# A recurrent mixer moved into a build-time plan, its conditioning sums moved from TensorE to VectorE

## The chip, the cores and the metric

One NeuronCore of a Trainium2 chip runs the whole program. The metric is the time of one execution in device microseconds; several executions give a median. The engines are named as in the profile: PE is TensorE's matmuls, PEld its weight loads, DVE is VectorE, ACT is ScalarE, POOL is GpSimd, SP is SyncE, which issues most of the transfers (DMAs) in one queue.

## The reference

Two transformer layers over 512 tokens of width 1024, in fp32. Layer 0 has a gated linear recurrence (HGRN2) as its mixer, layer 1 dilated attention; each layer then has a SwiGLU feed-forward. Six vectors per layer, computed from a conditioning vector, shift, scale and gate the normalised inputs and the outputs. Cut to what the change touches:

```python
cond = silu(c)                                             # [1, 1024]
for layer in range(2):
    mod = cond @ ada_w[layer] + ada_b[layer]               # [1, 6 * 1024]
    sh1, sc1, g1, sh2, sc2, g2 = split(mod, 6)             # vectors 0 to 5
    u = rms_norm(h, norm_g[layer, 0]) * (1 + sc1) + sh1
    y = hgrn2_mixer(u, ...) if layer == 0 else dilated_attention_mixer(u, ...)
    h = h + (1 + g1) * rms_norm(y, norm_g[layer, 1])
    u = rms_norm(h, norm_g[layer, 2]) * (1 + sc2) + sh2
    h = h + (1 + g2) * rms_norm(swiglu_ffn(u, ...), norm_g[layer, 3])

def hgrn2_mixer(u, w_in, lb, norm_g, w_out):               # 8 heads of 128, chunks of 32 tokens
    q_raw, f_raw, v, g = (u @ w_in) in four parts
    log_f = log(lb + (1 - lb) * sigmoid(f_raw)); k = (1 - lb) * sigmoid(-f_raw); q = silu(q_raw)
    b = cumsum(log_f within a chunk)
    o = tril((q * exp(b)) @ (k * exp(-b)).T) @ v + (q * exp(b)) @ state    # state decays from chunk to chunk
    return (rms_norm(o) * norm_g * silu(g)) @ w_out
```

## The kernel before

Weights come from HBM as a list of items (`items`), each about 1 MB, into "raw" tiles of 128 x 2048 fp32. The `Stream` class loads them in the list's order on SP's queue; two raw tiles take turns, so a load waits until the work on the item two places ahead is done. A weight item ("w") is split into a high part (a cast on ACT, L113) and a low part (a subtraction on DVE, L114), and every product is three matmuls (high x high, low x high, high x low; L599 to L601). Three pairs of such parts ("hi", "lo") are kept.

Between the weights the list has conditioning items ("ada"): half of the rows (`kq`) of a 512-column half (`hf`) of one vector `v` of layer `l`. During the recurrent mixer the list has 18 of them, for vectors (0, 2), (0, 4), (0, 3), (1, 4) and half of (1, 1). They are worked off in one of two ways:

- on TensorE, `ada_groups` (L386), for layer 0's vectors 2, 3 and 4: four matmuls of a 128 x 32 block of the conditioning vector, one for each quarter of the array's columns (L395), into a PSUM bank, which ACT copies to SBUF at the end (L399);
- on DVE, `ada_chunk` (L402), for the others: four instructions per item, each a chunk of 128 x 512 times a column of the conditioning vector, added to a sum in SBUF (L415 for the first, L417 for the rest).

The sum over the partitions is then taken by a matmul with ones (`sum_by_pe`: L444, L462) or by a GpSimd reduction, and "do" and "rows" items finish the vector.

The recurrent mixer starts once the values of all tokens are projected. For each of four pairs of heads it runs blocks of 128 output columns: two for the forget gate (sigmoids, L1631 and L1633), two for the query (L1641, L1642), and, for the pair before, two for the output gate (`gate_pair`, L1615 to L1618). Between the blocks come the steps of the recurrence, put off by a count of blocks (`Fillers`, `LAG`):

- `decays`: two scans on DVE (L1519, L1520) and products with them (L1523, L1524);
- `between` and `widened`: small products of decays, `ki` and `m64` on DVE (L1543, L1548, L1549), `k128` and `q128` on GpSimd (L1547, L1550);
- `core_a` to `core_d`: scores and mask, states of the chunks, outputs and their norm, and a transpose into `oT`.

Here the order on each engine is left to the framework's scheduler, which works from the program's order. Then `mixer_out` (L721) projects `oT` with the output weights: with `made=None` it opens the tiles for the high parts, cuts each head of `oT` in two (L594, L595) and runs the products of the first 512 columns for all tokens. From there on the order is written out by hand (`manual_schedule`).

The attention mixer of layer 1 is built in another way: its work is a list of tasks with an engine, a cost in us, and the names that they read and write (`Plan`, L164). `Plan.run` (L260) works out when each task is due, plays through 72 rules of choice, takes the one in which TensorE ends first, and emits the instructions in that order, which the engines then keep. There all conditioning is on DVE, the raw tiles are a place with two buffers, and the first products of the output projection are part of the plan.

Of the kernel before, what the change touches and what calls it, by code (L numbers as in the profile page):

```python
# [11 lines left out]
F32 = mybir.dt.float32  # L12
# [33 lines left out]
class Stream:  # L46
# [17 lines left out]
    def _load(self, i):  # L64
# [251 lines left out]
def block_kernel(tc, x, c, positions, ada_w, ada_b, norm_g, hgrn_w_in, lower, hgrn_norm_g, hgrn_w_out,  # L316
# [8 lines left out]
    with ExitStack() as ctx:  # L325
# [57 lines left out]
        by_pe = lambda l, v, hf: l == 0 and v in (2, 3, 4)  # L383
        sum_by_pe = lambda l, v, hf: by_pe(l, v, hf) or (l, v) == (1, 4) or (l, v, hf) == (1, 1, 0)

        def ada_groups(l, v, hf, kq):  # L386


            def run(raw):
                if kq == 0:  # L390
                    accs[l, v, hf] = bank("mm")
                ps, r = accs[l, v, hf], V4(raw)
                for k in range(4):
                    j = slice(32 * k, 32 * k + 32)
                    pe.matmul(ps[j], cond_tiles[:, kq * 4 + k], r[:, k], start=kq == 0, stop=kq == 1,  # L395
                              tile_position=(0, 32 * k))
                if kq == 1:
                    accs[l, v, hf] = acc_place()
                    act.copy(accs[l, v, hf], ps)  # L399
            return run  # L400

        def ada_chunk(l, v, hf, kq):  # L402
            if by_pe(l, v, hf):
                return ada_groups(l, v, hf, kq)

# [126 lines left out]
        items += weave(hg, own[:16] + [one[0], own[17] + one[1]], 1, 0.6) + hg_o[:1] + one[3][:1] + hg_o[1:]  # L532
        f0a, f0b = ffn_ws(0)
# [953 lines left out]

        otp = hx.enter_context(tc.tile_pool(name="h_ot", bufs=1))
# [5 lines left out]
        sc = cx.enter_context(tc.tile_pool(name="h_briefest", bufs=1))  # L1494
# [16 lines left out]
        bc = lambda a: a.unsqueeze(3).broadcast_to((P, 4, a.shape[2], 32))  # L1511

        def decays(hd, k, K, Q, dec):

            T = factors[k]
            act.activation(C33(T)[:, :, 1:33], C33(T)[:, :, 1:33], AF.Identity, scale=omlb[:, hd:hd + 1], bias=lb[:, hd:hd + 1])
            act.activation(K, K, AF.Copy, scale=omlb[:, hd:hd + 1])
            bb, suf = fresh(sc, [P, 528], "bb", 1), fresh(sc, [P, 528], "suf", 1)
            dve.tensor_tensor_scan(bb, T[:, 0:528], starts[:, 0:528], 0.0, op0=OP.mult, op1=OP.add)  # L1519
            dve.tensor_tensor_scan(suf[:, ::-1], T[:, 1:529][:, ::-1], starts[:, 1:529][:, ::-1], 0.0, op0=OP.mult, op1=OP.add)  # L1520
            dve.tensor_copy(dec[:, k], C33(bb)[:, :, 32])
            qd = fresh(sb, [P, S], "qd", 2)
            dve.tensor_mul(C16(qd), C33(bb)[:, :, 1:33], C16(Q))  # L1523
            dve.tensor_mul(C16(K), C33(suf)[:, :, 1:33], C16(K))  # L1524
            return qd, K

        def between(dec):

            d = dec.rearrange("p k (b c) -> p (k b) c", c=4)
            rdec = fresh(cp, [P, 2, 16], "rdec", 2)  # L1530
            dve.reciprocal(rdec, dec)
            dve.tensor_copy(reach[:, :, 1:7:5], d[:, :, 0:4:3])
            dve.tensor_mul(reach[:, :, 2:6:3], d[:, :, 0:3:2], d[:, :, 1:4:2])
            dve.tensor_mul(reach[:, :, 3:5], reach[:, :, 2:6:3], d[:, :, 2:0:-1])
            tot = fresh(cp, [P, 8, 1], "ftot", 2)
            dve.tensor_mul(tot, reach[:, :, 4:5], d[:, :, 0:1])
            dve.tensor_copy(f64[:, :, 0:4:3], d[:, :, 1:3])
            return rdec, tot

        def widened(hd, k, qd, ke, rdec, tot):  # L1540
            own = slice(4 * k, 4 * k + 4)
            ki = fresh(sc, [P, S], "ki", 2)
            dve.tensor_tensor(C16(ki), C16(ke), rdec[:, k].unsqueeze(2).broadcast_to((P, 16, 32)), op=OP.mult)  # L1543
            q128 = fresh(cp, [P, S], "q128", 2)
            k128 = fresh(sb, [P, S], "k128", 2)
            m64 = fresh(sc, [P, S], "m64", 2)
            pool.tensor_tensor(B44(k128), B44(ke), bc(reach[:, own, 4:8]), op=OP.mult)  # L1547
            dve.tensor_tensor(B44(m64)[:, :, 0:2], B44(ke)[:, :, 0:2], bc(f64[:, own, 0:2]), op=OP.mult)  # L1548
            dve.tensor_tensor(B44(m64)[:, :, 2:4], B44(qd)[:, :, 2:4], bc(f64[:, own, 2:4]), op=OP.mult)  # L1549
            pool.tensor_tensor(B44(q128), B44(qd), bc(reach[:, own, 0:4]), op=OP.mult)  # L1550
            return dict(qd=qd, ki=ki, ke=ke, q128=q128, k128=k128, m64=m64, tot=tot[:, own], hd=hd)

        def core_a(g):
            a = bank("a")
            qd, ki, ke, m64 = g["qd"], g["ki"], g["ke"], g["m64"]
            for o in range(0, S, P):
                pe.matmul(a[:, o:o + P], ki[:, o:o + P], qd[:, o:o + P], start=True, stop=True)
            for o in range(0, S, P):
                for s in (0, 64):
                    pe.matmul(a[s:s + 32, o + s + 32:o + s + 64], ke[:, o + s:o + s + 32],  # L1560
                              qd[:, o + s + 32:o + s + 64], start=True, stop=True, tile_position=(0, s))
            for o in range(0, S, P):
                pe.matmul(a[0:64, o + 64:o + P], m64[:, o:o + 64], m64[:, o + 64:o + P], start=True, stop=True,
                          tile_position=(0, 0))
            aT = fresh(cp, [P, NT, P], "aT", 2)
            dve.tensor_tensor(aT, V4(a), causal.unsqueeze(1).broadcast_to((P, NT, P)), op=OP.mult)
            g["aT"] = aT
            kb = bank("a")
            for b in range(NT - 1):
                pe.transpose(kb[:, b * P:(b + 1) * P], g["k128"][:, b * P:(b + 1) * P], ident)  # L1570
            act.copy(g["k128"][:, 0:384], kb[:, 0:384])

        def core_b(g):
            hs = slice(g["hd"] * P, (g["hd"] + 1) * P)
            kv = bank("b")
            for b in range(NT - 1):
                pe.matmul(kv[:, b * P:(b + 1) * P], g["k128"][:, b * P:(b + 1) * P], v_tok[:, b, hs], start=True, stop=True)
            sts = fresh(cp, [P, 3, P], "state", 1)
            act.copy(sts[:, 0], kv[:, 0:P])
            for b in (1, 2):  # L1580
                dve.scalar_tensor_tensor(sts[:, b], sts[:, b - 1], g["tot"][:, b], kv[:, b * P:(b + 1) * P],
                                         op0=OP.mult, op1=OP.add)
            g["sts"] = sts

        def core_c(g):
            hd = g["hd"]
            hs = slice(hd * P, (hd + 1) * P)
            ob = bank("b")
            for b in range(NT):
                sl = slice(b * P, (b + 1) * P)  # L1590
                pe.matmul(ob[:, sl], g["aT"][:, b], v_tok[:, b, hs], start=True, stop=b == 0)
                if b:
                    pe.matmul(ob[:, sl], g["q128"][:, sl], g["sts"][:, b - 1], start=False, stop=True)
            on = fresh(cp, [P, NT, P], "aT", 2).rearrange("p a b -> p (a b)")
            ss = fresh(cp, [P, 4], "oss", 2)
            for b in range(NT):
                act.activation(V4(on)[:, b], V4(ob)[:, b], AF.Square, accum_out=ss[:, b:b + 1])
            r = fresh(cp, [P, 4], "orr", 2)
            rstd_of(r, ss, P, cp, 4)
            dve.tensor_tensor(V4(on), V4(ob), r.unsqueeze(2).broadcast_to((P, 4, P)), op=OP.mult)  # L1600
            g["on"] = on

        def core_d(g):
            hd = g["hd"]
            tb = bank("a")
            for b in range(NT):
                pe.transpose(tb[:, b * P:(b + 1) * P], g["on"][:, b * P:(b + 1) * P], ident)
            act.activation(oT[hd], tb, AF.Copy, scale=hng[:, hd:hd + 1])

        def gate_pair(p):  # L1610
            whi, wlo = st.take()
            for k in range(2):
                ps = block(whi, wlo, k * P, 256)
                sg = fresh(qp, [P, S], "Q", 2)
                act.activation(PLACED(sg), SEEN(ps), AF.Sigmoid)  # L1615
# [4 lines left out]
            if p == 3:  # L1620
                fl.drain()

        LAG = 2
        fl.n = 0
        for p in range(4):
            tiles = []
            whi, wlo = st.take()
# [771 lines left out]
```

## Time and profile before

| | us |
|---|---|
| median of 3 runs | 1453.28 |
| lowest and highest run | 1449.09, 1457.71 |
| the profiled execution | 1450.59 |
| its span, first to last instruction | 1448.8 |
| busy PE, DVE, ACT, POOL | 1419.5, 1093.8, 808.5, 195.2 |
| recurrent mixer, from the end of the value products to the end of the first half of its output products | 72 to 288 |

The granted TensorE clock is full throughout. A group of instructions is given as line, engine, operation, tile written <- tiles read, shape, count, then busy time, mean ns of one, and the idle time of the engine before them with what ended it. A row of the timeline is start, duration, engine, line, operation, count. A row of waits is who waited <- for whom: us in total, times, longest. A matmul's recorded duration overlaps the next one's, so the pace of matmuls is read from their starts.

### The profile page before, as it was taken

The numbers are of one execution on the slowest core, as the hardware profiler recorded it, in microseconds if no ns is written. First come the engines' busy times: TensorE is split into PE (matmuls) and PEld (weight loads), VectorE is DVE, ScalarE is ACT, GpSimd is POOL, SyncE is SP. The second block draws the span as 40 slices with busy tenths as digits, with TensorE's granted clock in tenths as the row PEclk, the third lists the DMA queues.
The fourth block names the chain that finished last, engine by engine and source line by source line (L and its number), as shares of the span: only waits on it lengthen the run. The fifth ranks groups of instructions, "written<-read, shape, count | busy, mean of one in ns | idle before, by whom it ended". The sixth has DMA issues, their size and how long they took to land. (4 is left out here: it accounts for less than half of the span.)

```text
span 1448.8 us, 25264 instructions
## 1 busy us (share of the span) xinstructions
PE 1419.5 (98%) x9903; PEld 1306.6 (90%) x9903; DVE 1093.8 (75%) x1718; ACT 808.5 (56%) x1494; POOL 195.2 (13%) x179
## 2 busy tenths in 40 slices
PE   8999999999999999999999999999999999999998
PEld 6777888889999998888998999999988899999887
DVE  4567488488888889778797977888776978887644
ACT  4434443374555553366648878467885555555332
POOL 1011012040111103230000110001012211110100
PEclk9999999999999999999999999999999999999999
DMA  9656564113344458515244343344362334434541
GB/s 308 186 188 208 168 197 173 59 60 91 113 117 118 117 202 297 176 59 175 92 141 130 111 131 90 94 153 131 96 197 94 104 102 117 117 110 153 175 146 59
DMA packets 212872, 201.10 MB, mean 139 GB/s; under 512 B 8920, under 2 KB 170640, under 8 KB 212496
## 3 DMA queue, kind: packets, MB, share of 16 engines
q1 hardware_dynamic: 209776, 192.71, 42.8%
q10 hardware_dynamic: 1952, 6.65, 1.2%
q8 instruction: 78, 1.28, 0.4%
q0 software_dynamic: 1024, 0.12, 0.2%
q14 instruction: 42, 0.34, 0.1%
HBM read 192.30 MB, written 5.30 MB: 136 GB/s over the span
## 5 line engine op out<-in xcount | busy, mean ns | idle before, releaser
L1860 PE MATMUL ps_mm<-apart,hiq 128*128 128x256 f32 (+1 forms) x608 | 137.3, 320 | 1.3 <-ACT hiq L1995 0.8
L114 DVE TENSOR_TENSOR lo<-raw,hi 128x2048 fp32r<-128x2048 f32 x39 | 95.2, 2440 | 49.8 <-ACT hi L113 49.7
L599 PE MATMUL ps_mm<-uh,hi 128*128 128x512 f32 (+1 forms) x368 | 130.2, 354 | 0.0
L600 PE MATMUL ps_mm<-ul,hi 128*128 128x512 f32 (+1 forms) x368 | 128.4, 349 | 1.6 <-DVE ul L699 1.6
L113 ACT CAST hi<-raw 128x2048 fp32r<-128x2048 f32 x39 | 74.3, 1905 | 97.1 <-DMA raw<-in_ffn_w_out_dram 31.9
L601 PE MATMUL ps_mm<-uh,lo 128*128 128x512 f32 (+1 forms) x368 | 128.1, 348 | 0.0
L1860 PEld LDWEIGHTS ps_mm<-apart,hiq 128*128 128x128 f32 x608 | 99.9, 191 | 7.5 <-ACT xs L1974 1.0
L971 DVE TENSOR_TENSOR loq<-raw,hiq 128x1024 fp32r<-128x1024 f32 x72 | 85.0, 1221 | 20.1 <-ACT hiq L967 20.1
L980 PE MATMUL ps_mm<-th,hiq 128*128 128x256 f32 x360 | 99.1, 275 | 0.0
L980 PE MATMUL ps_mm<-tl,hiq 128*128 128x256 f32 x360 | 99.0, 275 | 0.0
L980 PE MATMUL ps_mm<-th,loq 128*128 128x256 f32 x360 | 99.0, 275 | 0.0
L1860 PE MATMUL ps_mm<-apart,loq 128*128 128x256 f32 (+1 forms) x304 | 95.4, 314 | 0.6 <-DVE loq L1996 0.6
L951 POOL TENSOR_TENSOR raw<-raw 128x512 f32<-128x512 f32 x36 | 47.8, 1329 | 320.0 <-DVE spare L947 165.2
L967 ACT CAST hiq<-raw 128x1024 fp32r<-128x1024 f32 x72 | 72.1, 1046 | 20.9 <-DVE raw L955 16.3
L599 PEld LDWEIGHTS ps_mm<-uh,hi 128*128 128x128 f32 x368 | 69.9, 190 | 12.4 <-issue 4.4
L599 PE MATMUL ps_mm<-hi,oh 128*128 128x512 f32 x208 | 79.0, 381 | 0.0
L600 PE MATMUL ps_mm<-lo,oh 128*128 128x512 f32 x208 | 78.9, 379 | 0.0
L600 PEld LDWEIGHTS ps_mm<-ul,hi 128*128 128x128 f32 x368 | 69.9, 190 | 9.3 <-DVE ul L699 2.0
L1083 ACT CAST oh<-mid 128x512 fp32r<-128x512 f32 x44 | 37.2, 868 | 69.9 <-PE ps_b L600 61.4
L601 PEld LDWEIGHTS ps_mm<-uh,lo 128*128 128x128 f32 x368 | 69.9, 190 | 6.7
L1860 PE MATMUL ps_mm<-uh,hiq 128*128 128x256 f32 x256 | 71.3, 278 | 0.2 <-ACT ps_mm L1949 0.2
L1860 PE MATMUL ps_mm<-uh,loq 128*128 128x256 f32 x256 | 70.5, 275 | 0.2 <-DVE loq L1907 0.2
(474 smaller groups left out, 4729.8 us busy)
## 6 DMA issues: line engine op xcount, KB each, us to landing
raw<-in_ada_w_dram SPq DMA_DIRECT2D x40, 1024.0 KB, 6.3
raw<-in_ffn_w_in_dram SPq DMA_DIRECT2D x144, 256.0 KB, 4.1
raw<-in_ffn_w_out_dram SPq DMA_DIRECT2D x22, 1024.0 KB, 6.8
raw<-in_attn_w_in_dram SPq DMA_DIRECT2D x64, 256.0 KB, 4.3
raw<-in_hgrn_w_in_dram SPq DMA_DIRECT2D x12, 1024.0 KB, 5.4
raw<-in_attn_w_in_dram SPq DMA_DIRECT2D x12, 1024.0 KB, 5.1
raw<-in_ffn_w_in_dram SPq DMA_DIRECT2D x8, 1024.0 KB, 5.0
raw<-in_attn_w_in_dram SPq DMA_DIRECT2D x16, 512.0 KB, 5.0
```

The lines of the kernel that those rows point to most:

```text
L113: self.nc.scalar.copy(hi, t)
L114: self.nc.vector.tensor_sub(lo, t, hi.bitcast(F32))
L599: pe.matmul(ps, ah, bh, start=start, stop=False, skip_group_check=part)
L600: pe.matmul(ps, ah, bl, start=False, stop=False, skip_group_check=part)
L601: pe.matmul(ps, al, bh, start=False, stop=stop, skip_group_check=part)
L951: pool.tensor_add(r[:, 2], r[:, 2], r[:, 0])
L967: act.copy(hi, src)
L971: dve.tensor_sub(lo, src, hi.bitcast(F32))
L980: pe.matmul(LAID(ps), w[x][:, a], TAKE(us[kt][y]), start=begin and kt + m == 0, stop=kt == 3 and m == 2, skip_group_check=True)
L1083: act.copy(PLACED(oh), SEEN(mid(f)))
L1860: pe.matmul(LAID(dst()), x, TAKE(y), start=begin and i == 0, stop=i == len(todo) - 1, skip_group_check=True)
```

## The change

1. `ada_groups` and `by_pe` go: all conditioning items take the four DVE instructions. The sums over partitions stay where they were.
2. The planning helpers of the attention mixer (`PE`, `ACT`, `DVE`, places, loads, `condition`, `next_weights`) become a function, `planner(extra, end)`, which both mixers call. `condition` learns the sum by matmul.
3. The recurrent mixer becomes tasks of such a plan: blocks as four products tasks of six matmuls each, the steps of the recurrence with a cost for each instruction, weight splits in two halves of 1024 columns. The first products of the output projection (all of the first 512 columns, and seven eighths of the next bank) join the plan, and `mixer_out` goes on from them.
4. A third raw tile, `third`, is opened for this mixer and used for items up to the end of its output weights (`behind`). Each raw tile is now a place of its own (`raw0`, `raw1`, `raw2`), and each load's place waits for the place of the load before it, so that loads keep the list's order.
5. The pool of the shortest-lived tiles (`scx`) closes on its own, before the tiles of the output projection are opened; these wait for the last head's scores and all tasks ahead of them.

```diff
-    def _load(self, i):
+    def _load(self, i, place=None):
...
+        elif place is not None:
+            t = place
...
-        by_pe = lambda l, v, hf: l == 0 and v in (2, 3, 4)
-        sum_by_pe = lambda l, v, hf: by_pe(l, v, hf) or (l, v) == (1, 4) or (l, v, hf) == (1, 1, 0)
-        def ada_groups(l, v, hf, kq):
...
+        sum_by_pe = lambda l, v, hf: (l, v) in ((0, 2), (0, 3), (0, 4), (1, 4)) or (l, v, hf) == (1, 1, 0)
...
+        behind = len(items)
...
+        def planner(extra=(), end=0):
...
+            def load_next():
+                spot = seq[0] % (2 + len(extra))
+                seq[0] += 1
+                while st.items[to_load[0]][1] is None:
+                    to_load[0] += 1
+                if spot >= 2 and to_load[0] >= end:
+                    return
+                to_load[0] += 1
...
+                    st._load(st.loaded, extra[spot - 2] if spot >= 2 else None)
...
+                p = plan.place(f"raw{spot}", 1, make)
+                if queue_order:
+                    plan.tasks[-1]["deps"].add(queue_order.pop())
+                queue_order.append(len(plan.tasks) - 1)
+                plan.add("DMA", 3.4, None, w=[p()], late=2.2)
+                queue.append(p)
...
+            def condition(item):
...
+                    for k in range(4):
...
+                        DVE(0.68, chunk, [raw()], [a()])
...
+                if kind == "do" and sum_by_pe(l, v, hf):
...
+                    PE(0.46, to_cols, [a()], [b()])
+                    DVE(0.2, lambda: col_done(l, v, slice(hf * 4, hf * 4 + 4), b.t[:, 0:4]), [b()])
...
+        third = qp.tile([P, 2048], F32, name="third")
+        plan, ... = planner((third,), behind)
...
+        def splits():
...
+            for n in range(2):
+                two = slice(n * 1024, n * 1024 + 1024)
+                ACT(0.96, lambda two=two: act.copy(p.t[0][:, two], raw.t[:, two]), [raw()], [p("h", n)])
+                DVE(1.15, lambda two=two: dve.tensor_sub(p.t[1][:, two], raw.t[:, two], p.t[0][:, two].bitcast(F32)), [raw(), p("h", n)], [p("l", n)])
+            done_with_raw()
...
+        def whole_block(p, k):
+            b = mm_of()
+            for part in range(4):
...
+                products(6 * 0.2159, lambda: b.t, b(), terms, part == 0, [p("h", part // 2), p("l", part // 2)])
...
+            DVE(1.17, lambda: dve.tensor_tensor_scan(bb.t, ...), [T(0), T(1)], [bb()])
+            DVE(1.15, lambda: dve.tensor_tensor_scan(suf.t[:, ::-1], ...), [T(0), T(1)], [suf()])
...
+            POOL(1.25, lambda: pool.tensor_tensor(B44(k128.t), B44(ke.t), bc(reach[:, own, 4:8]), op=OP.mult), [ke(), ("reach", 0)], [k128()])
+            DVE(0.34, lambda: dve.tensor_tensor(B44(m64.t)[:, :, 0:2], ...), [ke(), ("f64", 0)], [m64(0)])
+            DVE(0.34, lambda: dve.tensor_tensor(B44(m64.t)[:, :, 2:4], ...), [qd(), ("f64", 0)], [m64(1)])
+            POOL(1.25, lambda: pool.tensor_tensor(B44(q128.t), B44(qd.t), bc(reach[:, own, 0:4]), op=OP.mult), [qd(), ("reach", 0)], [q128()])
...
+        t = plan.add(None, 0.0, lambda e: (scx.close(), out_parts(aux, oh, KT, "left")), [], [opened])
+        plan.tasks[t]["deps"].update(range(of_core[-1] + 1))
...
+        with tc.manual_schedule(engines=ORDERED | {mybir.EngineType.SP}):
+            planned = plan.run()
+        st.done, st.taken = at_item[0], st.taken + len(steps) + 4
+        made = aux, oh, ol, [b.t for b in y0], {0: y1[0].t}, [p.t for p in ws[2:]]
+        first = mixer_out(oT, otp, gates.pop((0, 2)).t, 0, "left", cx.close, made)
-        first = mixer_out(oT, otp, gates.pop((0, 2)), 0, "left", lambda: None)
```

More of the change, by code (lines that the diff above doesn't have):

```diff
@@ L1754, in block_kernel @@
         dve.tensor_tensor(maskR[:, P:256], maskR[:, 0:P], lqf, op=OP.min)
-        plan = Plan()
-        ticks, clock = Fillers(), [0.0]
-        at_item, places_of = [st.done], {}
-        ready_first = list(range(len(st.ready)))
+        plan, ticks, at_item, ready_first, of_units, mm_of, slot, PE, ACT, DVE, POOL, COPY, done_with_raw, next_weights, split_place, products, condition = planner()
         Q = lambda t, k, n=1: t[:, k * 512:(k + n) * 512]
@@ L1844, in next_weights @@
-        def next_weights():
-            while True:
-                item = st.items[at_item[0]]
-                at_item[0] += 1
-                if item[0] in ("w", "quarters", "half"):
-                    return queue.pop(0)
-                condition(item)
-        def split_place(first):
-            return plan.place("hl", 3, lambda: st.part_tiles(first))
-        def products(cost, dst, key, terms, begin, reads):
-            def go():
-                todo = [p for t in terms() for p in t]
-                for i, (x, y) in enumerate(todo):
-                    pe.matmul(LAID(dst()), x, TAKE(y), start=begin and i == 0, stop=i == len(todo) - 1, skip_group_check=True)
-            of_units.append(len(plan.tasks))
-            PE(cost, go, reads, [key])
```

492 lines of the change are left out of this document (284 added, 208 removed).

## The prediction

> **What bounds the kernel now.** I read the page from the top: busy time by engine, then the mixer's stretch cut into windows, then the spacing of matmuls, then waits.
>
> ```profile
> span 1448.8 us, 25264 instructions
> PE 1419.5 (98%) x9903; PEld 1306.6 (90%) x9903; DVE 1093.8 (75%) x1718; ACT 808.5 (56%) x1494; POOL 195.2 (13%) x179
> ```
>
> TensorE has work in flight for 98% of the span, so the end is set by how many matmuls there are and how closely they follow. The execution that this profile shows took 1450.59 us, 1.8 outside the span; the median of the three runs is 1453.28 (1449.09 to 1457.71), 2.7 above it. I sum against 1450.59.
>
> The change lies in the recurrent mixer: from the end of the value products (72 us) to the end of the first half of its output projection (288). The windows of that stretch (columns: length; busy time of PE, PEld, DVE, ACT, POOL; clock, DMA share, GB/s):
>
> ```profile
> 72.00:180.00 108.00, 106.62 (x670) 85.03 (x669) 66.33 (x97) 44.39 (x95) 13.99 (x19) 1.00 0.57 189
> 180.00:240.00 60.00, 58.90 (x366) 51.88 (x365) 55.21 (x90) 21.80 (x44) 13.79 (x11) 1.00 0.54 176
> 240.00:288.00 48.00, 48.00 (x299) 42.91 (x298) 22.95 (x33) 17.06 (x38) 2.01 (x2) 1.00 0.32 109
> sum 216.00, PE 213.51 PEld 179.82 DVE 144.49 ACT 83.25 POOL 29.80; mean PE 71.17 PEld 59.94 DVE 48.16 ACT 27.75 POOL 9.93
> ```
>
> TensorE is idle for 2.5 of 216 us, at full clock. VectorE is busy for 144.5, but unevenly: 61% until 180, 92% from 180 to 240, 48% after. Whatever is added to VectorE before 240 meets that middle stretch.
>
> TensorE's waits there, all of them:
>
> ```profile
> PE ps_b L1593 <- DVE state L1581: 1.1, 1, 1.1
> PE ps_a L1607 <- DVE aT L1600: 0.9, 1, 0.9
> PE ps_b L462 <- ACT shared L399: 0.4, 1, 0.4
> ```
>
> 2.4 us in three waits, none on a load: order written by a planner can win little from waits here. The gain must come from matmuls taken out.
>
> **The change part by part.**
>
> *Conditioning leaves TensorE.* Twelve of the 18 conditioning items of this stretch (vectors 2, 3, 4 of layer 0) are now eight packed passes each on TensorE:
>
> ```profile
> L395 PE MATMUL ps_mm<-raw,cond_tiles 128*32 128x512 f32 x96 | 12.4, 602 | 0.2
> ```
>
> A busy time says nothing on spacing, so here is the timeline around one item (start, duration):
>
> ```profile
> 84.33 0.38 PE L599 MATMUL ps_mm<-uh,hi 128*128 128x512 f32 x1
> 84.55 0.38 PE L600 MATMUL ps_mm<-ul,hi 128*128 128x512 f32 x1
> 84.76 0.38 PE L601 MATMUL ps_mm<-uh,lo 128*128 128x512 f32 x1
> 85.07 1.07 PE L395 MATMUL ps_mm<-raw,cond_tiles 128*32 128x512 f32 x8
> 86.07 0.48 PE L599 MATMUL ps_mm<-uh,hi 128*128 128x512 f32 x1
> 86.39 0.38 PE L600 MATMUL ps_mm<-ul,hi 128*128 128x512 f32 x1
> ```
>
> Ordinary products start 0.216 us apart though each lasts 0.38. From the product at 84.76 to the one at 86.39 are 1.63 us where two spacings (0.43) would do: 1.20 for an item standing alone. Two pairs of items stand back to back and cost a little less. Bounds: 12 x 1.0 (the spacing inside alone) to 12 x 1.2, 12.0 to 14.4; I take **13.6**. ScalarE's six evictions of these sums go too; ScalarE is busy for 83 of 216 us, so that is worth nothing, except the 0.4 us wait on L399 above.
>
> *It arrives on VectorE.* Each item becomes four chunk instructions of 128x512: 48 in all, 6 of the first kind, 42 of the second. The same lines run on VectorE already for the other items:
>
> ```profile
> L417 DVE SCALAR_TENSOR_TENSOR shared<-raw,cond,shared 128x512 f32<-128x512 f32 x21 | 17.3, 823 | 2.7 <-DMA raw<-in_ada_w_dram 2.4
> L415 DVE TENSOR_SCALAR shared<-raw,cond 128x512 f32<-128x512 f32 x3 | 2.2, 742 | 0.0
> 192.16 2.32 DVE L417 SCALAR_TENSOR_TENSOR shared<-raw,cond,shared 128x512 f32<-128x512 f32 x3
> 195.00 0.74 DVE L417 SCALAR_TENSOR_TENSOR shared<-raw,cond,shared 128x512 f32<-128x512 f32 x1
> ```
>
> By mean durations that is 42 x 0.82 + 6 x 0.74 = 39 us. Three in a row take 2.32 where one takes 0.74, so in a row they follow at 0.79: 48 x 0.79 = 38. At the least, if all ran like the last row, 35. I take **37**, all of it before the last weight tile is split, that is before about 240. No matmul needs it at once: sums of vectors 3 and 4 serve the feed-forward after this stretch. What it can delay is what stands behind it in VectorE's queue: weight splits and the recurrent steps.
>
> *Splits in halves.* 14 weight tiles are split as two 1024-column pieces instead of one:
>
> ```profile
> L114 DVE TENSOR_TENSOR lo<-raw,hi 128x2048 fp32r<-128x2048 f32 x14 | 32.1, 2290 | 29.0 <-ACT hi L113 29.0
> L134 DVE TENSOR_TENSOR lo<-raw,hi 128x1024 fp32r<-128x1024 f32 x10 | 11.8, 1217 | 1.8 <-ACT hi L133 1.8
> ```
>
> 14 x (2 x 1.22 - 2.29) = +2 us of VectorE. Against it, VectorE now waits 29.0 us for whole casts on ScalarE; halves let it start a cast sooner. That wait is idle time that the new work can use.
>
> *VectorE's account.* 144.5 + 37 + 2 = 183 us, in a stretch that is 216 - 16 = 200 if everything is won: 92%. Up to 240 it is 121.5 + 37 + 1 = 160 us in 152. So not all can be won in the old order: some 8 us of VectorE work must move past 240, where VectorE idles for 25 of 48 us. Steps of the last two heads, which the planner may postpone while TensorE runs gate blocks, are of that kind.
>
> *Planned order.* The stretch gets the planner that the attention stage has. Nothing shows the mixer under it; the nearest row is that stage:
>
> ```profile
> sum 400.00, PE 392.52 PEld 374.08 DVE 323.84 ACT 286.48 POOL 35.53; mean PE 98.13 PEld 93.52 DVE 80.96 ACT 71.62 POOL 8.88
> PE ps_a L2164 <- DMA qk<-shared: 2.2, 1, 2.2
> PE ps_mm L1860 <- DVE loq L2042: 2.1, 4, 0.7
> ```
>
> (700 to 1100 us.) TensorE idles for 7.5 us of 400, 1.9%, with VectorE at 81%. Over 200 us that is 3.7. With VectorE at 92% its slack is less than half (8% for 19%), so I more than double it: **8 us** of new waits, in place of the 2.4 of now. Bounds: 0 (a planner that meets none) and 37 (each of the 12 items holds TensorE up by its own 3.1). 8 is nearer to the attention row, whose planner, buffers and kinds of wait are the same.
>
> *Third raw tile and the order of loads.* A conditioning tile is held for about 3 us on VectorE instead of 1.0 on TensorE, and the next load on SP's queue stands behind its release, as do all later loads:
>
> ```profile
> SPq L85 <- PE ps_mm L395: 40.0, 12, 10.2
> ACT hi L113 <- DMA raw<-in_hgrn_w_in_dram: 31.2, 8, 6.3
> ```
>
> Twelve loads waited for that release, and casts waited 31 us for loads, yet no matmul waited for either. Two microseconds longer, twelve times, are 24 us on a chain of two tiles; a third tile gives a whole load time back each round, and the DMA engines are at 0.57. Bounds: -1 (late casts) to +8 (a third of the 24 not covered). I take 0; if the cover were gone, ScalarE's casts, VectorE's splits and TensorE would be late in turn.
>
> *Output projection in the plan, attention on the shared factory.* The same matmuls, cuts and loads; no wait is in the last window now (PE 48.00 of 48.00). For attention only the tile's names differ and the load order stays: 0 for both, bounds -1 and +2 each.
>
> **Sum:** 1450.6 - 13.6 - 2.4 + 8 = 1442.6; I give **1443**.
>
> **The rivals.**
>
> *A: the gain stays in part.* As summed, 1437 to 1446.
>
> *B: the planner finds room for everything.* No new wait: 1450.6 - 16 = 1434.6. For it: VectorE's 29 us behind casts and 25 us after 240 are usable. Against: 160 us of VectorE work in 152.
>
> *C: VectorE and GpSimd stand in each other's way, and VectorE becomes the bound.* From two timelines (start, duration) and the groups (after the bar: busy, mean ns of one, idle before):
>
> ```profile
> 133.23 0.41 DVE L1548 TENSOR_TENSOR m<-K,f 128x256 f32<-128x256 f32 x1
> 133.57 1.27 DVE L1549 TENSOR_TENSOR m<-qd,f 128x256 f32<-128x256 f32 x1
> 134.76 1.27 DVE L1548 TENSOR_TENSOR m<-K,f 128x256 f32<-128x256 f32 x1
> 134.51 1.23 POOL L1550 TENSOR_TENSOR q<-qd,reach 128x512 f32<-128x512 f32 x1
> L1550 POOL TENSOR_TENSOR q<-qd,reach 128x512 f32<-128x512 f32 x8 | 10.0, 1246 | 11.2 <-DVE qd L1523 5.2 <-PE ps_b L1593 4.8 <-DVE cols L435 1.2
> L1547 POOL TENSOR_TENSOR k<-K,reach 128x512 f32<-128x512 f32 x8 | 9.7, 1207 | 62.2 <-DVE reach L1534 62.2
> L1549 DVE TENSOR_TENSOR m<-qd,f 128x256 f32<-128x256 f32 x8 | 6.6, 830 | 0.1
> L1548 DVE TENSOR_TENSOR m<-K,f 128x256 f32<-128x256 f32 x8 | 5.9, 734 | 0.0
> ```
>
> The same 0.41 us instruction takes 1.27 beside GpSimd and ends with it. GpSimd's 16 products are 19.7 us; if VectorE, now dense, loses all of them instead of part (8 x 0.42 + 8 x 0.32 = 6 on the last two lines), its load rises by up to 13 to 196 of 200. New waits would then be about 8 + 8 (the part of the 13 that falls before 240): 1450.6, no change. The Trainium skill (SBUF — State Buffer, section Who interferes with whom) says that a VectorE instruction with two SBUF inputs contends with a GpSimd one that reads SBUF, and that the loser is blocked for the whole instruction. The rows above agree (1.27 against 0.41). By that rule each new chunk, which reads raw and sum from SBUF, is exposed, and the time would be C's.
>
> *D: slower.* VectorE works strictly in order. If a split or recurrent step that TensorE needs next stands behind the four chunks of an item, TensorE idles for up to 3.1 us. Twelve new items that all do it cost 37: 1472. It decides from the point where six do (18.6 over the 16 won); with eight, 1459; with nine, 1462. For it: 160 in 152. Against: 55 of 60 us busy from 180 to 240 now, and one 1.1 us wait.
>
> *That the change does not do what it says* would show as L395 still on TensorE; the text leaves no call of it, so this gets no chance.
>
> **How the numbers follow.** A 0.50, B 0.08, C 0.25, D 0.17. About 0.5% (7.3 us) is what a measurement of this kernel can tell from no change: faster is below 1446.0, slower above 1460.5. A and B are faster less 0.03 for A's upper end: 0.55; C with that and D's lower end: 0.29; slower 0.16. The likeliest time is A's, 1443, its own range 1437 to 1446. For 8 in 10 the range goes from 1434 (B) to 1459 (C, and D with eight items).
>
> **What would show it.** No L395 on TensorE and 13 to 14 us fewer from 72 to 288; the chunk line 66 to 72 times on VectorE there, and VectorE at 175 to 190 us; TensorE's waits 4 to 12 us, most of them on VectorE; SP's loads released by VectorE's sums, and no matmul behind a load. Wrong would be: TensorE idle over 16 us (D), chunks at over 1 us on average (C), or a stage past 288 that changed by more than 2.

## The result and the profile after

| | us | ratio to before (95% interval) |
|---|---|---|
| before, median of 5 | 1451.87 | |
| after, median of 5 | 1440.51 (1436.47 to 1440.64) | 0.9909 [0.9881, 0.9936] |
| after, the profiled execution | 1437.54 | |

The changed kernel is faster by 11.4 us in the medians and by 13.1 us between the two profiled executions. 1443 had been forecast, as a sum on the profiled execution of before (1450.59). The profiled execution of after is 1437.54, 3.0 below its median.

The head of the page of the changed kernel, then its windows of the mixer's stretch (same columns as before):

```profile
span 1435.7 us, 25151 instructions
PE 1406.7 (98%) x9807; PEld 1304.7 (91%) x9807; DVE 1119.5 (78%) x1780; ACT 807.5 (56%) x1502; POOL 204.9 (14%) x179
```

```profile
72.00:180.00 108.00, 105.85 (x641) 93.36 (x640) 97.99 (x160) 45.33 (x101) 25.08 (x22) 1.00 0.59 196
180.00:240.00 60.00, 60.00 (x416) 53.82 (x415) 55.18 (x92) 22.36 (x51) 12.12 (x8) 1.00 0.51 176
240.00:288.00 48.00, 47.55 (x253) 42.13 (x252) 29.62 (x51) 24.71 (x62) 7.54 (x7) 1.00 0.26 88
sum 216.00, PE 213.40 PEld 189.31 DVE 182.79 ACT 92.39 POOL 44.74; mean PE 71.13 PEld 63.10 DVE 60.93 ACT 30.80 POOL 14.91
```

These windows have the same bounds as before, but the changed kernel is 14.4 us ahead at their end, so 182.8 us for VectorE has some of the next stage in it. The same work as in before's 72 to 240 and 240 to 288 lies in these two windows:

```profile
72.00:225.60 153.60, 151.45 (x932) 134.20 (x931) 139.07 (x228) 62.33 (x141) 32.74 (x28) 1.00 0.56 186
225.60:273.60 48.00, 48.00 (x303) 43.02 (x302) 32.05 (x52) 19.32 (x43) 8.16 (x4) 1.00 0.45 154
```

For that work VectorE is busy for 171.1 us (139.1 and 32.1) where it was busy for 144.5 (121.5 and 23.0): 85% of a stretch that is now 201.6 us long. TensorE has 96 matmuls fewer and the same few us of idle time. All its waits from 72 to 290 (the second belongs to the norm behind the output projection):

```profile
PE ps_a L1797 <- DVE aT L1787: 2.2, 1, 2.2
PE ps_b L663 <- DVE xn L657: 0.4, 1, 0.4
```

To compare kernels I use one distance on the timeline: from the last value product to the first transpose of the output projection's hand-ordered part. It was 222.8 us (73.02 to 295.81) and is 208.8 (72.63 to 281.41): 14.0 of the gain are won there. The two ends, before and after:

```profile
295.81 1.04 PE L680 MATMUL ps_b<-ident,xn 128*128 128x128 f32 x8
281.41 1.04 PE L663 MATMUL ps_b<-ident,xn 128*128 128x128 f32 x8
```

After is still 14.35 us ahead at the end of the first feed-forward (627.31 and 612.96). The attention stage gives about 1.2 back, of which more below.

The loads and the casts, from the same view of waits (SPq is the queue of loads):

```profile
SPq L87 <- DVE shared L1547: 61.7, 12, 11.0
...
ACT hiq L1649 <- DMA raw<-in_hgrn_w_in_dram: 14.7, 5, 5.8
```

Twelve loads are released by VectorE's sums, as foreseen, and casts wait for loads about half as long as before (17.0 with the 2.3 us for the third tile, against 31.2).

### The profile page after: what moved, and what is told of

Read it like the earlier page. It is cut to its first block, busy times and chain, and to the rows that moved or that the text cites. A ratio compares the mean times of both kernels' runs of the same rounds, so it can differ in the third digit from the quotient of the medians.

```text
span 1435.7 us, 25151 instructions
## 1 busy us (share of the span) xinstructions
PE 1406.7 (98%) x9807; PEld 1304.7 (91%) x9807; DVE 1119.5 (78%) x1780; ACT 807.5 (56%) x1502; POOL 204.9 (14%) x179
## 3 DMA queue, kind: packets, MB, share of 16 engines
q0 software_dynamic: 1024, 0.12, 0.2%
## 5 line engine op out<-in xcount | busy, mean ns | idle before, releaser
L1600 PE MATMUL ps_mm<-uh,hiq 128*128 128x256 f32 (+1 forms) x416 | 134.6, 323 | 0.5 <-ACT ps_mm L2067 0.5
L1600 PE MATMUL ps_mm<-uh,loq 128*128 128x256 f32 (+1 forms) x416 | 131.2, 315 | 0.2 <-DVE loq L2025 0.2
L1600 PE MATMUL ps_mm<-ul,hiq 128*128 128x256 f32 (+1 forms) x416 | 131.0, 315 | 0.0
L1600 PEld LDWEIGHTS ps_mm<-uh,hiq 128*128 128x128 f32 x416 | 79.4, 191 | 5.1 <-ACT ps_mm L2067 0.9
L1600 PEld LDWEIGHTS ps_mm<-uh,loq 128*128 128x128 f32 x416 | 79.4, 191 | 4.7 <-DVE loq L2025 0.4
L1600 PEld LDWEIGHTS ps_mm<-ul,hiq 128*128 128x128 f32 x416 | 79.4, 191 | 4.1 <-issue 0.5
L116 DVE TENSOR_TENSOR lo<-raw,hi 128x2048 fp32r<-128x2048 f32 x25 | 63.2, 2527 | 21.5 <-ACT hi L115 21.5
L963 PEld LDWEIGHTS ps_mm<-th,loq 128*128 128x128 f32 x360 | 69.1, 192 | 0.0
L963 PEld LDWEIGHTS ps_mm<-tl,hiq 128*128 128x128 f32 x360 | 69.1, 192 | 0.0
L963 PEld LDWEIGHTS ps_mm<-th,hiq 128*128 128x128 f32 x360 | 69.1, 192 | 0.0
```

Source lines behind the costliest of these rows:

```text
L116: self.nc.vector.tensor_sub(lo, t, hi.bitcast(F32))
L963: pe.matmul(LAID(ps), w[x][:, a], TAKE(us[kt][y]), start=begin and kt + m == 0, stop=kt == 3 and m == 2, skip_group_check=True)
L1600: pe.matmul(LAID(dst()), x, TAKE(y), start=begin and i == 0, stop=i == len(todo) - 1, skip_group_check=True)
```

## The experiments

Theory: the twelve items' passes on TensorE are the gain, and the planned order lets VectorE take them over almost free. Rivals: the planned order alone is the gain; or any order would do, since VectorE had the time; or the third tile carries it.

### Order without the move, move without the order

`e2`: the changed kernel with the twelve items as packed passes on TensorE again, as tasks of the plan.

```diff
+                    if l == 0 and v in (2, 3, 4):
...
+                                pe.matmul(ps.t[j], cond_tiles[:, kq[0] * 4 + k], r[:, k], start=kq[0] == 0, stop=kq[0] == 1,
+                                          tile_position=(0, 32 * k))
+                        PE(1.0, groups, [raw()], [ps()])
```

> The changed kernel, with the 12 items of layer 0's vectors 2, 3 and 4 back on TensorE as tasks of the plan (eight packed passes each, and an eviction on ScalarE per sum); plan, third raw tile and the rest as changed. T: the 13.6 us come back, less up to 2 because VectorE is lighter: 1450 to 1454, no change from before. R1: it stays fast, 1439 to 1443. R2 says as T.

1452.19 us against 1452.94 of before: 0.9998 [0.9984, 1.0011]. Its windows' sum:

```profile
sum 216.00, PE 215.84 PEld 181.85 DVE 148.64 ACT 87.04 POOL 31.34; mean PE 71.95 PEld 60.62 DVE 49.55 ACT 29.01 POOL 10.45
```

TensorE is without a gap, the stretch is 220.2 us: the planned order, with the third tile and the halves, is worth 2.6 us of trace by itself (the old waits were 2.4), which the medians can't tell from nothing. The rival "the order is the gain" falls.

`e1`: the kernel before, all conditioning on VectorE, in the framework's order and with two raw tiles.

```diff
-        by_pe = lambda l, v, hf: l == 0 and v in (2, 3, 4)
+        by_pe = lambda l, v, hf: False
```

> The kernel before, with one edit: all 18 conditioning items of the mixer run on VectorE; order by the framework's scheduler, two raw tiles. Theory T (TensorE's removed passes are the gain, and the plan is what lets VectorE carry the items without holding TensorE up): 13.6 us less of matmuls, but 5 to 14 us of new TensorE waits on VectorE, so 1443 to 1451. Rival R1 (the planned order is itself the gain, the move is neutral): 1450 to 1454. Rival R2 (VectorE has so much room that any order will do): waits of TensorE under 4 us and 1438 to 1442, as in the changed kernel.

1463.85 us, 1.0076 [1.0048, 1.0103]: slower, which my theory had not expected either; the move without the order loses more than the move with it wins. The stretch is 234.8 us and has 16.5 us of TensorE waits in it, more than the 13.6 that left. VectorE is busy for 172.2 us from 72 to 288. Its longest wait, VectorE's timeline ahead of it (start, duration), and a window in it (the figure before DMA share and GB/s is the granted clock):

```profile
PE ps_b L1591 <- DVE state L1581: 5.3, 1, 5.3
```

```profile
135.53 2.28 DVE L114 TENSOR_TENSOR lo<-raw,hi 128x2048 fp32r<-128x2048 f32 x1
137.73 1.53 DVE L417 SCALAR_TENSOR_TENSOR shared<-raw,cond,shared 128x512 f32<-128x512 f32 x1
139.18 0.68 DVE L1642 TENSOR_TENSOR Q<-Q,ps_mm 128x512 f32<-128x512 f32 x1
...
139.85 0.33 DVE L1581 SCALAR_TENSOR_TENSOR state<-state,ftot,ps_b 128x128 f32<-128x128 f32 x1
```

```profile
138.00:141.00 3.00, 0.00 (x0) 0.00 (x0) 3.00 (x7) 0.00 (x0) 1.70 (x2) 0.66 0.68 183
```

The 0.33 us state update that TensorE needs stands behind a split, a chunk (1.53 us here, beside a product of GpSimd) and a gate product. That is rival D's mechanism. "Any order would do" falls: under the plan such waits stay away. Two more things add to it: the clock falls (0.66 in this window), and two tiles are now too few, as casts wait longer for loads:

```profile
ACT hi L113 <- DMA raw<-in_hgrn_w_in_dram: 72.4, 9, 11.6
```

(31.2 before.) How much of the 12 us belongs to the order and how much to the two tiles is not separated here; `e3` has two tiles under the plan and bounds it.

### The third tile, the order of loads, the halves

`e3`: the changed kernel without the third tile.

```diff
-        third = qp.tile([P, 2048], F32, name="third")
-        plan, ... = planner((third,), behind)
+        plan, ... = planner()
```

> The changed kernel without the third raw tile: two tiles take turns in the mixer. T: loads stand further from TensorE than a load takes, so 0 to +2 us against the changed kernel: 1440 to 1443, and no matmul behind a load. Rival R3 (the third tile is what pays for VectorE holding a tile three times as long): ScalarE's casts wait for loads over 30 us as in the kernel before, splits come late, TensorE waits 6 to 15 us more: 1446 to 1456.

1442.04 us, 0.9927 [0.9902, 0.9953]; the stretch is 211.4. Under the plan the third tile is worth 2.6 us of trace, no more; the medians do not tell the two kernels apart.

`e8`: the changed kernel without the wait of each load for the load before it, in both plans. Some tiles then hold another item than the one meant, so the kernel computes something else; its time is that of the same instructions on other data.

```diff
-                    plan.tasks[-1]["deps"].add(queue_order.pop())
+                    queue_order.pop()
```

> The changed kernel with the wait of each load's place for the one before it taken out of both plans; the places then take the list's items in the order in which the plan opens them, so some tiles hold another item than the one meant (the time is that of the same instructions on other data). T and R1: the wait for one another costs nothing, as SP's queue runs far ahead: 1440 within 3. A rival, that the fixed order holds back a load that the plan would have had sooner: 3 to 6 us faster than the changed kernel.

1442.33 us, 0.9931 [0.9908, 0.9954]; the stretch 208.2, one wait of 1.4 us in the mixer. Keeping the loads in order costs nothing that can be seen: without it the time is no better.

`e9`: splits in one piece of 2048 columns, as before the change.

```diff
-            for n in range(2):
-                two = slice(n * 1024, n * 1024 + 1024)
-                ACT(0.96, ...)
-                DVE(1.15, ...)
+            both = [p("h", 0), p("h", 1)]
+            ACT(1.82, lambda: act.copy(p.t[0], raw.t), [raw()], both)
+            DVE(2.21, lambda: dve.tensor_sub(p.t[1], raw.t, p.t[0].bitcast(F32)), [raw()] + both, [p("l", 0), p("l", 1)])
```

> The changed kernel with each weight tile split by one cast and one subtraction of 128x2048 in the plan (costs 1.82 and 2.21), as in the kernel before, instead of halves. If the planned order is what lets VectorE carry the items: 1440 to 1444. If the halves are (VectorE begins a split one cast of 1.9 us sooner, 14 times): VectorE waits 15 to 25 us for casts, TensorE 5 to 12 us, 1446 to 1453.

1439.22 us, 0.9913 [0.9897, 0.9929], the changed kernel's own ratio. No wait at all is left in its mixer, and the stretch is 206.5. So halves are not needed, and this kernel gives the sum its parts: `e2` to `e9`, neither with a wait over 0.2 us in the mixer, is 220.2 - 206.5 = 13.7 us for the twelve items; before to `e2` is 2.6 for the old waits; `e9` to after is 2.3 for the one new wait.

### How full may VectorE be?

`e4` and `e5`: one and two idle chunks more per conditioning item (18 and 36 instructions of 128x512, into a tile that nobody reads; the second kernel has `k < 2`).

```diff
                         DVE(0.68, chunk, [raw()], [a()])
+                        if extra and k < 1:
...
+                            DVE(0.68, again, [raw()], [("void", 0)])
```

> The changed kernel with one idle chunk instruction more for each of the mixer's 18 conditioning items (128x512, two inputs from SBUF, into a scratch tile that nobody reads; 0.68 us in the plan). VectorE in the mixer goes from 183 to 195 us of some 202. Theory T2 (the planned order can run VectorE nearly full, so TensorE loses time only once VectorE's load passes what the stretch has): 1440 to 1444. Rival Q (waits grow steadily with VectorE's load, as the prediction had it: 8 us at 92%): +4 to +8, 1445 to 1449.

> As the run before, with two idle chunks more per item: 36 in all, VectorE at 207 of 202 us. T2: it is now the bound, and the overrun and little more is paid: +5 to +12 against the changed kernel, 1446 to 1453. Rival S (conditioning can be put off, so VectorE does not bind): within 2 of the changed kernel, 1439 to 1443. Q: +12 to +16, 1453 to 1457.

`f2`: 5.5 us less on VectorE, the product of each head's output norm on ScalarE instead.

```diff
-            DVE(0.6, lambda: dve.tensor_tensor(on.t, V4(ob.t), r.t.unsqueeze(2).broadcast_to((P, 4, P)), op=OP.mult), ...)
+            for b in range(NT):
+                ACT(0.26, lambda b=b: act.activation(on.t[:, b], V4(ob.t)[:, b], AF.Copy, scale=r.t[:, b:b + 1]), [ob(), r()], [on(b)])
```

> The last product of each head's output norm (one 128x512 on VectorE, 0.69 us, eight times) becomes four 128x128 scalings on ScalarE: VectorE loses 5.5 us, ScalarE gains some 9. Theory (TensorE bounds the stretch, VectorE fits at 92%): freeing VectorE brings no more than the one wait, 0 to 2.3 us, so 1437.5 to 1441. Rival (waits grow steadily with VectorE's load, and some of the spacing on TensorE is hidden waiting): 5.5 us less VectorE brings 3 us or more, below 1437.

`f0`: the changed kernel again, beside `f2`.

> The changed kernel once more, as the measure for the three kernels beside it: 1436 to 1441, with one wait of about 2 us in the mixer and the stretch from the last value product to the first transpose of the output projection at 208 to 210 us.

| | durations of VectorE's work against after | VectorE busy in the stretch | stretch | median | ratio |
|---|---|---|---|---|---|
| `f2` | -5.5 us | 174.1 | 207.7 | 1437.93 | 0.9903 [0.9885, 0.9921] |
| after (`f0`) | 0 | 176.0 | 208.5 | 1439.05 | 0.9913 [0.9895, 0.993] |
| `e4` | +14.3 (8.3 + 6.0 in the groups) | 187.8 | 214.4 | 1446.32 | 0.9967 [0.9952, 0.9981] |
| `e5` | +27.5 (15.6 + 11.9) | 199.9 | 227.7 | 1457.83 | 1.0039 [1.0025, 1.0053] |

The time bends: 5.5 us less bring 0.8, 14 more cost 5.9, and the next 13 cost 13. I had hoped that `e4` would be free, since after has 14.8 us of VectorE left before 240 (153.2 of 168 us busy); it was not, and both `e4` and `e5` came out at the times of rival Q, or a little above. TensorE's waits in the mixer grow nearly steadily, as Q says: 1.9, 5.2 and 10.4 us in `f0`, `e4` and `e5`. Nor is VectorE's time used up: before 240 it is idle for 10.8 us in `e4` and 10.1 in `e5`. Later loads, which tiles held longer might cause, do not show as a cause: ScalarE's casts wait for loads for 12.2 and 9.5 us there, less than in after (17.0).

In `e5` these waits are 8.5 us longer than in `f0`, but the stretch grows by 19.2. Windows of it show where more is lost:

```profile
204.00:207.00 3.00, 1.78 (x16) 1.59 (x15) 2.18 (x4) 2.59 (x12) 0.01 (x1) 1.00 0.00 0
207.00:210.00 3.00, 2.16 (x8) 1.54 (x8) 2.83 (x4) 2.66 (x5) 1.00 (x1) 0.87 0.04 8
210.00:216.00 6.00, 6.00 (x18) 5.09 (x19) 5.85 (x11) 0.00 (x0) 0.00 (x0) 0.50 0.76 236
```

Two waits of 1.5 and 0.6 us lie between 204 and 210. From 210 the granted clock is 0.50 and TensorE, busy throughout, gets 18 matmuls into 6 us.

### VectorE and GpSimd

`e6`: the 16 products `k128`, `q128` on VectorE instead of GpSimd.

```diff
-            POOL(1.25, lambda: pool.tensor_tensor(B44(k128.t), B44(ke.t), ...
+            DVE(0.61, lambda: dve.tensor_tensor(B44(k128.t), B44(ke.t), ...
-            POOL(1.25, lambda: pool.tensor_tensor(B44(q128.t), B44(qd.t), ...
+            DVE(0.61, lambda: dve.tensor_tensor(B44(q128.t), B44(qd.t), ...
```

> The changed kernel with the two widened products per head (k128, q128) on VectorE instead of GpSimd: 16 x 0.6 = 10 us more work there. If the two engines stand in each other's way: the m and ki lines go back to 0.41 and 0.68 us, the 4x128 power on GpSimd to 1.0 us at every place (2.3 us at one place now), VectorE's busy time rises by 1 to 4 us only, and the time is 1437 to 1441. If they do not: VectorE rises by 10 and the time is 1441 to 1446.

The groups of the changed kernel from 72 to 300 (VectorE, then GpSimd), and two of `e6`:

```profile
L1547 DVE SCALAR_TENSOR_TENSOR shared<-raw,cond,shared 128x512 f32<-128x512 f32 x32 | 24.7, 773 | 0.1
L1547 DVE SCALAR_TENSOR_TENSOR shared<-third,cond,shared 128x512 f32<-128x512 f32 x31 | 24.4, 787 | 0.2
...
L1715 DVE TENSOR_TENSOR ki<-K,rdec 128x512 f32<-128x512 f32 x8 | 8.2, 1026 | 0.0
L1718 DVE TENSOR_TENSOR m<-K,f 128x256 f32<-128x256 f32 x8 | 5.7, 707 | 0.0
L1720 DVE TENSOR_TENSOR m<-qd,f 128x256 f32<-128x256 f32 x8 | 4.2, 519 | 0.0
...
L1722 POOL TENSOR_TENSOR q<-qd,reach 128x512 f32<-128x512 f32 x8 | 15.3, 1910 | 4.1 <-DVE qd L1692 4.1
L1786 POOL TENSOR_TENSOR orr<-rv,expo 128x4 f32<-128x4 f32 x8 | 12.2, 1519 | 90.0 <-DVE rv L1785 90.0
L1717 POOL TENSOR_TENSOR k<-K,reach 128x512 f32<-128x512 f32 x8 | 11.5, 1442 | 46.0 <-DVE reach L1704 32.5 <-DVE K L1693 13.3 <-POOL orr L1786 0.2
```

```profile
L1715 DVE TENSOR_TENSOR ki<-K,rdec 128x512 f32<-128x512 f32 x8 | 5.5, 682 | 0.0
...
L1718 DVE TENSOR_TENSOR m<-K,f 128x256 f32<-128x256 f32 x8 | 3.2, 405 | 0.0
```

So the lock is there: without GpSimd's products `ki` falls from 1026 to 682 ns and `m` (L1718) from 707 to 405. But in the changed kernel VectorE loses no more by it than before on these lines, 8 x 0.344 + 8 x 0.302 + 8 x 0.11, about 6 us on `ki` and the two `m`, against 6 on the two `m` then; GpSimd loses more, its 16 products taking 26.8 us instead of 19.7. The timeline of after shows both ways (VectorE rows, then GpSimd's of the same times):

```profile
106.13 0.68 DVE L1715 TENSOR_TENSOR ki<-K,rdec 128x512 f32<-128x512 f32 x1
106.73 0.41 DVE L1718 TENSOR_TENSOR m<-K,f 128x256 f32<-128x256 f32 x1
...
107.40 2.35 DVE L1650 TENSOR_TENSOR loq<-raw,hiq 128x1024 fp32r<-128x1024 f32 x2
...
129.26 1.27 DVE L1718 TENSOR_TENSOR m<-K,f 128x256 f32<-128x256 f32 x1
...
137.50 0.69 DVE L1787 TENSOR_TENSOR aT<-ps_b,orr 128x512 f32<-128x512 f32 x1 [0.91 <-POOL orr L1786]
```

```profile
105.68 6.08 POOL L1722 TENSOR_TENSOR q<-qd,reach 128x512 f32<-128x512 f32 x1 [4.09 <-DVE qd L1692]
128.74 1.50 POOL L1717 TENSOR_TENSOR k<-K,reach 128x512 f32<-128x512 f32 x1
135.14 2.33 POOL L1786 TENSOR_TENSOR orr<-rv,expo 128x4 f32<-128x4 f32 x1 [3.71 <-DVE rv L1785]
```

At 105.68 GpSimd starts a product of 1.25 us and needs 6.08, while VectorE's instructions from 106.13 to 109.75 run at their undisturbed times; at 129 it is the other way round (`m` 1.27). The Trainium skill (SBUF — State Buffer, section Who interferes with whom) says that the order of issue, not the operation, decides who is blocked. The rows agree: at 105.68 an instruction of VectorE is under way (from 105.52), at 129.26 GpSimd's product (from 128.74). How full VectorE's queue is does not decide it, as it has no gap at either place; why GpSimd gets no turn between VectorE's instructions until 109.75 is open. The rows also show where the one new wait comes from: the power of 128x4 at 135.14 takes 2.33 us where an undisturbed one takes 1.0, `aT` comes late, and TensorE's transpose waits 2.2 us for it; 1.3 of these are the power's.

Yet `e6` is no gain: 1446.12 us, 0.9967 [0.9951, 0.9982], a stretch of 215.0. The lock had let me expect 1437 to 1441, and VectorE's busy time in the stretch did not even rise (175.4 us against 175.9 in after). The power still takes 1.25 us on average, so something else delays it too; other instructions of VectorE are likely, but not tried. Its one long wait, with VectorE's rows ahead of it, and windows behind it:

```profile
240.04 0.17 DVE L1785 TENSOR_SCALAR rv<-oss 128x4 f32<-128x4 f32 x1 [2.33 <-ACT aT L1783]
...
243.78 0.75 DVE L1547 SCALAR_TENSOR_TENSOR shared<-third,cond,shared 128x512 f32<-128x512 f32 x1
244.43 0.69 DVE L1787 TENSOR_TENSOR aT<-ps_b,orr 128x512 f32<-128x512 f32 x1
```

```profile
245.27 1.09 PE L1797 MATMUL ps_a<-ident,aT 128*128 128x128 f32 x4 [4.54 <-DVE aT L1787]
```

```profile
243.00:249.00 6.00, 3.73 (x18) 3.76 (x19) 5.97 (x13) 5.52 (x10) 0.00 (x0) 0.50 0.08 11
249.00:252.00 3.00, 3.00 (x9) 2.55 (x10) 3.00 (x4) 0.64 (x1) 0.00 (x0) 0.50 0.95 335
252.00:255.00 3.00, 3.00 (x17) 2.62 (x17) 1.58 (x3) 0.00 (x0) 0.00 (x0) 0.81 0.95 330
```

GpSimd's power is done at 241.36 (1.01 us, undisturbed), but `aT` stands behind five more instructions of VectorE until 244.43: TensorE waits 4.5 us, 3.1 of them for this queue, and the clock is then 0.50 for some 8 us of its work. For the planner, VectorE has 16 x 0.61 = 9.8 us more to do here, as its costs for `ki` and `m` (0.6 and 0.34 us) are the undisturbed ones in both kernels. Why its order puts `aT` behind those five is not shown.

`f1`: the planner is told 2.3 us for the power instead of 1.0.

```diff
-            POOL(1.0, lambda: pool.tensor_tensor(r.t, rv.t, expo[:, 0:4], op=OP.pow), [rv()], [r()])
+            POOL(2.3, lambda: pool.tensor_tensor(r.t, rv.t, expo[:, 0:4], op=OP.pow), [rv()], [r()])
```

> The planner is told 2.3 us, as measured in the changed kernel's trace, for GpSimd's power of 128x4 instead of 1.0; nothing else is edited. If the one new 2.2 us wait of the changed kernel comes from that power running longer beside a dense VectorE than the plan allowed for (lock theory), the plan starts it earlier: no wait at that place, the stretch 206 to 207 us instead of 208.8, median 1437 to 1439. If the wait is only where the plan's small errors happen to add up (drift theory), another of the same size stands elsewhere and the time does not move: 1439 to 1441.

1439.78 us, 0.992 [0.9902, 0.9938]; the stretch is 208.3. These are the numbers of the drift theory: no gain, and a wait of 1.6 us elsewhere. At the transpose that waited 2.2 us in after (1.9 in `f0`, 0.8 in `f2`) the power now takes 1.12 us and TensorE waits no more. The new wait is at the transpose before it. VectorE's rows, then TensorE's:

```profile
127.15 1.57 DVE L1715 TENSOR_TENSOR ki<-K,rdec 128x512 f32<-128x512 f32 x1
128.64 1.27 DVE L1718 TENSOR_TENSOR m<-K,f 128x256 f32<-128x256 f32 x1
129.83 1.26 DVE L1720 TENSOR_TENSOR m<-qd,f 128x256 f32<-128x256 f32 x1
131.02 0.68 DVE L1787 TENSOR_TENSOR aT<-ps_b,orr 128x512 f32<-128x512 f32 x1
131.84 0.63 PE L1797 MATMUL ps_a<-ident,aT 128*128 128x128 f32 x4 [1.64 <-DVE aT L1787]
```

The plan with the new cost put `aT` behind `ki` and two `m`, and here the lock hits VectorE: the three take 2.6 us more than their undisturbed 0.68, 0.41 and 0.41. So the lock is behind both waits, once by GpSimd's loss and once by VectorE's, and one corrected cost only moves it. With whole splits (`e9`) the wait is gone, but the medians do not show it: no kernel here is measurably faster than the changed one.

### One more thing off TensorE

`f3`: as `f2`, and the sums over partitions of vectors (0, 3), (0, 4), (1, 4) and half of (1, 1) by GpSimd.

```diff
-        sum_by_pe = lambda l, v, hf: (l, v) in ((0, 2), (0, 3), (0, 4), (1, 4)) or (l, v, hf) == (1, 1, 0)
+        sum_by_pe = lambda l, v, hf: (l, v) == (0, 2)
```

> The same, and the sums over partitions of vectors (0,3), (0,4), (1,4) and half of (1,1) leave TensorE (56 products with ones, 5.8 us by spacing) for GpSimd reductions with four small VectorE steps each, so VectorE has about 5 us more than in the changed kernel. Theory (every pass taken off TensorE pays as long as VectorE fits): 208.8 - 5.8 and the wait, a stretch of 201 to 204 us, 1432 to 1436. Rival (the lock between VectorE and GpSimd: seven reductions of several us each block VectorE, or are held up and come late, and VectorE is already full up to 240): no gain or a loss, 1440 to 1450.

1476.06 us, 1.017 [1.015, 1.019]; the stretch is 244.3. Worse than the rival, and for the most part not by the lock. GpSimd's timeline:

```profile
136.32 3.25 POOL L1550 PARTITION_ALL_REDUCE shared<-shared  x1 [5.67 <-PE ps_mm L1600]
147.12 1.05 POOL L1786 TENSOR_TENSOR orr<-rv,expo 128x4 f32<-128x4 f32 x1 [7.55 <-issue]
```

```profile
PE ps_a L1797 <- ACT aT L1788: 19.0, 3, 9.1
PE ps_a L1749 <- POOL k L1717: 7.8, 2, 4.7
```

The reductions themselves take 3.3 to 5.9 us, against 3.3 in the plan. But after each of the seven, GpSimd's next instruction of another kind starts 6.8 to 12.3 us later, four times with nothing that it waits for ("issue"), and before each it is idle for at least 5.7. The power or `k128` comes that much later, and with it the head's transpose or the product that needs `k128`: 19.0 and 7.8 us of waits in five places, and the clock after them (0.93 over the stretch).

## Why the prediction was right

By its steps:

- **Conditioning leaves TensorE, 13.6.** Measured 13.7 (`e2` to `e9`). Right.
- **It arrives on VectorE: 37 us, an account of 183 us, 92% of the stretch.** The chunk line stands there 72 times (63 on L1547, 9 on L1545), as forecast, but the account was 12 us too high: 171.1 us, 85%. It added recorded durations to busy time. In a full queue each duration overlaps the next instruction's start (106.13 + 0.68 lies behind 106.73 above), so over that work the durations add up to 33.7 us more than before, but the busy time is only 26.6 us longer. That 182.8 from 72 to 288 looks like the forecast is chance.
- **Old waits, 2.4.** 2.6 between before and `e2`. Right.
- **New waits, 8.** 2.3: the term that was mis-sized. On the profiled executions, on which it was summed, the forecast was 5.1 us too high (1442.6 against 1437.54), and this term alone was 5.7 too high. That the median of after lies 3.0 above its profiled execution brings the number nearer to 1443, by luck. I scaled the attention stage's idle share up for a VectorE at 92%. It was at 85%, and that stage's rows do not tie its waits to a full VectorE: the longest is on a transfer. The mixer itself went nearly as rival B said, while the time lies in A's range. What I held against B, 160 us of work in 152, was 139.1 in 153.6. About as much work did move to the stretch's last 48 us as I had said must, 32.1 us lie there, where 23.0 did.
- **The signs.** TensorE's waits were to be 4 to 12 us. They were 2.2 in the stretch, so this sign was missed.
- **Third tile and load order, 0.** No matmul waits for a load; `e8` shows no cost of the order, and `e3` that the third tile covers 2.6 us.
- **Halves: +2 us on VectorE, against idle time behind casts.** VectorE waits 3.5 us for casts instead of 29.0; but with whole splits `e9` is as fast and has 4.9 us of this wait, so the plan and not the halves found that time.
- **Attention, 0, bounds -1 and +2.** Its length in the traces is 453.1 us before and 453.9 in `e1`, which has the old code for it, and 454.4 after. In the eleven other kernels with the shared planner it is 454.7 to 456.9. So a part of the 1.2 us, or more, seems to belong to the change, near the upper bound; what causes it is open.

The rivals: C's lock is real, but GpSimd bore the additional loss (VectorE loses about 6 us on its three lines, as before; GpSimd's products take 26.8 us instead of 19.7), and VectorE stayed clear of being the bound. D's mechanism is real too: `e1` shows it where no plan stands against it. Its chance of 0.17 was for a planned order; without one it would have been the right forecast.

## What to carry to other kernels

Work may leave the engine that bounds a stage for one that is then busy for 85% of it, if the order on that engine is planned together with the rest; the same move in a scheduler's order can cost as much as it could have won. Leave the target engine slack: here the move itself brought 2.3 us of waits, 14 us more of work cost 5.9, and 13 more cost 13, where TensorE's clock fell too, although VectorE still had 10 us of idle time ahead of the point where its results are needed. Count that load by the starts of instructions, not by adding durations, and compare stages by the work in them, not by fixed times. A cost in a planner is worth checking against the trace for what stands between instructions too, as with GpSimd's reductions.

## What the runs showed of the hardware that I had not expected

- **A wait can be paid twice.** After 4.5 us without matmuls the granted clock was 0.50 for about 8 us of dense work (`e6`); after two waits of 1.5 and 0.6 us close together it was 0.50 for 6 us (`e5`); after a single one of 2.2 us it stayed at 1.00 (after). The Trainium skill (TensorE: Matmul & The Clock Gate, Part 1) has the clock halved after an idle window of about 3.4 us and back after as much busy time. `e6` agrees with the first half of that; the case of `e5` and the time until full speed returns do not come out of it, and the runs don't give a threshold.
- **Either engine can lose the lock, and GpSimd for several instructions in a row.** A GpSimd product of 1.25 us took 6.08 at one place; at another VectorE's `ki` of 0.68 took 1.57 (`f1`).
- **GpSimd's reduction over partitions had 6.8 us and more behind it** before another kind of instruction started, seven times of seven (`f3`).
